# Sixteen tiles of an input projection by a form of Strassen's product, and two attention chains in lockstep

## The chip, the cores and the metric

One core of a Trainium2 chip runs the kernel. Five engines work from queues of their own: TensorE (PE) multiplies, VectorE (DVE), ScalarE (ACT) and GpSimd (POOL) work elementwise, SyncE (SP) issues the transfers. Semaphores order them. The metric is the time of one execution in device microseconds (us); lower is better. Before the change three runs gave 994.83 to 1002.69 us with a median of 996.45.

## The reference

One layer of a decoder trunk for 1024 tokens of width 1024: an input projection of the normed x, softmax attention on latents (MLA), gated linear attention (GLA) with 4 heads in chunks, a gated merge, an output product and gated embeddings.

```python
h = rmsnorm(x, norm_in_g[l])
proj = h @ w_in[l]
(cq, ckv, kr, gate_mla, gq, gk, gv, gk_low, gate_gla, merge_a, merge_b) = split_in(proj)
...
o_mla = mla_attention(q_nope, q_rope, k_nope, k_rope, v_mla).reshape(b, s, MLA_WIDTH)
y_a = (o_mla * jax.nn.silu(gate_mla)) @ w_mla_br[l]
...
o_gla = gla_chunked(qg, kg, vg, log_a).astype(x.dtype)
o_gla = rmsnorm(o_gla, gla_norm_g[l]).reshape(b, s, GLA_DV)
y_b = (o_gla * jax.nn.silu(gate_gla)) @ w_gla_br[l]
merged = jax.nn.sigmoid(merge_a) * y_a + jax.nn.sigmoid(merge_b) * y_b
x = x + merged @ w_out[l]
```

## The kernel before

Activations lie transposed, features on the 128 partitions and tokens along the row, in two halves of 512 tokens. Every float32 operand of a dense product is split into a high part that PE takes in one pass (fp32r) and the rest: `split` (L126) rounds the high part on ACT and subtracts on DVE. A product is then three matmuls, `mm3` (L144 to L147): high x high, and the two mixed ones; so all dense matmuls of the kernel stand in three lines.

The input projection has 33 tiles of 128 features. `stream` (L158) loads a tile's weights (`wr`, 512 KB, then `wh` and `wl`) one tile ahead; `bank` (L149) makes one PSUM bank of it: 8 k-tiles x 3 matmuls of 128x128 by 128x512, for one half of the tokens, so two banks of 24 a tile. An evict function takes the bank off PSUM times the tokens' rstd `rb` (L466): GG is GLA's gate (sg), GM the other gate, MA and MB the merge gates (stored to d_ta and d_tb in HBM), CKV and CQ the latents.

Linear attention, `gla(t, h)` (L531), works on head pair t and token half h in 11 steps: decayed keys and chunk states, then chunk scores transposed, level by level (exponents `level`, on DVE and ACT; `cross`, L559, 8 small matmuls into a two-bank tile L; `put`, L641, DVE's predicated copy into `at`), the outputs `o`, their norm, and the transposes `oT` back, multiplied into sg. The state runs from half 0 to half 1, so each head pair is a chain of two. `steps` (L733) runs the four one after the other, and after each of the 44 steps the loop asks `fill`, a stream of 29 of the tiles, for one bank. The rest of `fill` covers the splits of sg and the `finish_latent` (L757) of ckv and cq: broadcast of their norm's factor by PE (`dg`, `rb`) and 10 splits (`ch`, `cl`). Then come the softmax attention with `yb`, GLA's branch product, as filler, and the merge.

The written order gives priorities and data; a scheduler at build time fixes each engine's order, so the order of instructions is read from the built program. Work tiles come from 35 slots (`alloc`, `drop`, first in first out); a load waits on SP until its slot's last reader is done, and everything behind it on SP waits too.

```python
for _ in steps():
    next(fill)
    n_left -= 1
```

Of the kernel before, what the change touches and what calls it, by code (L numbers as in the profile page):

```python
# [8 lines left out]
F32 = mybir.dt.float32  # L9
# [42 lines left out]

def hybrid_kernel(tc, a, out):
# [3 lines left out]
    with ExitStack() as ctx:  # L57
# [7 lines left out]
        free = list(range(NSLOT))  # L65
        held = {}
        pools = [sp, None]
# [62 lines left out]
        def split_gain(dst_hi, dst_lo, src, g):  # L130
            """the two parts of src * g, g per partition"""
# [12 lines left out]
        def mm3(ps, lh, ll, rh, rl, first, last):  # L144
            nc.tensor.matmul(ps, lh, rh, start=first, stop=False)  # L145
            nc.tensor.matmul(ps, lh, rl, start=False, stop=False)  # L146
            nc.tensor.matmul(ps, ll, rh, start=False, stop=last)  # L147

        def bank(get, hi, lo, w, c0, kts, xh, xl, h, evict, tag="d"):  # L149
            """out[w features, half h of the tokens] with the weights' k-tiles at c0 + kt * w."""  # L150
            ps = get(tag, "d")
            n = len(kts)
            for i, kt in enumerate(kts):
                c = slice(c0 + kt * w, c0 + kt * w + w)
                mm3(ps[:w], hi[:, c], lo[:, c], xh[kt][:, hs(h)], xl[kt][:, hs(h)], i == 0, i == n - 1)
            evict(h, ps)

        def stream(get, jobs, xh, xl, primed=None, ahead=1, order=None):  # L158
# [17 lines left out]
            for n, h in order:  # L176
# [3 lines left out]
                bank(get, *ws[n], w, 0, range(nk), xh, xl, h, evict)  # L180
# [6 lines left out]
        def newton(dst, ss, n, w):  # L187
            """dst = rsqrt(ss / n + EPS), [128, w]"""
# [14 lines left out]
        def newton1(dst, s1, s2, n):  # L203
            """dst = rsqrt((s1 + s2) / n), [128, 1]; v is half the argument, the iterates change sign"""
# [13 lines left out]
        def rstd_rows(get, tag, acc, n, r):  # L218
            """From acc[128, tokens] (sums of squares by partition) the rstd of token block tb in r[128, 8]."""
# [5 lines left out]
        def rstd_parts(r):  # L225
            """both parts of r [128, 8]"""
# [5 lines left out]
        def rstd_bcast(get, tag, parts, h):  # L232
            """[128, 512] in PSUM: rstd of each token of half h along the free axis, on every partition."""
# [17 lines left out]
        d_rq = [[dr.tile([P, S], F32, name=f"d_rq{g}{y}") for y in range(2)] for g in range(2)]  # L251
        d_zb = [dr.tile([P, S], F32, name=f"d_zb{m}") for m in range(8)]
# [19 lines left out]
        with tc.tile_pool(name="ps0", bufs=1, space=PSUM) as ps0:  # L272
# [20 lines left out]
            # the array reaches its full clock only under load: it gets some while the first loads are on their way  # L293
# [4 lines left out]
            # x * g in two parts, and the sums of squares  # L298
            nc.sync.dma_start(wm0, a["w_misc"][:, 0 : NVEC + 128])
            xh, xl, xT = [], [], []  # L300
            acc = [alloc(F32, "xacc"), alloc(F32, "xacc")]
            first = stream(get, jobs, xh, xl)
            for k in range(8):
# [10 lines left out]
                xh.append(alloc(F32R, f"xh{k}"))  # L314
# [1000 lines left out]
```

## Time and profile before

| | |
|---|---|
| runs (3) | 994.83 to 1002.69 us, median 996.45 |
| profiled execution | span 995.6 us, 13955 instructions |
| PE busy | 968.8 us, 97% |
| DVE busy | 585.0 us, 59% |
| ACT, POOL busy | 413.4 us (42%), 127.8 us (13%) |
| longest wait of PE | 5.2 us, for kl in the softmax attention |

The span is the time from the first to the last instruction of the one profiled execution; the sum of the prediction is made against it. Busy times are unions over an engine's instructions. Matmuls run into one another, so a duration of one is longer than the time from its start to the next start. Idle time of PE in a stretch is the length less the busy time there.

### The profile page before, as it was taken

Reading aid. Unit: us, or ns where it says so; the run is one execution under the profiler, and the core shown is the slowest. Engines: PE = TensorE matmul, PEld = TensorE weight load, DVE = VectorE, ACT = ScalarE, POOL = GpSimd, SP = SyncE. Lnnn points to the kernel's source line nnn. Section 1 sums busy time; section 2 is a strip of 40 time slices with the busy share of each in tenths; the row PEclk is TensorE's granted clock in tenths of the full one; section 3 lists DMA queues with packets and bytes.
Section 4 is the critical chain, followed back from the end, with each engine's and each line's share of the span. In section 5 each row is a group of like instructions: output and inputs, shape, how many; then the busy total and the mean of one; then the engine's idle time right before and its main releaser. Section 6 shows DMA issues by size and latency. Waiting matters only on the chain. (4 is left out here: it accounts for less than half of the span.)

```text
span 995.6 us, 13955 instructions
## 1 busy us (share of the span) xinstructions
PE 968.8 (97%) x5152; PEld 801.1 (80%) x5152; DVE 585.0 (59%) x1219; ACT 413.4 (42%) x800; POOL 127.8 (13%) x103
## 2 busy tenths in 40 slices
PE   7999999999999999999999999997999999999996
PEld 5787778887887788788888788886888778889985
DVE  6727764375364355342567568885756862238766
ACT  7316721332331332221233246785886432237333
POOL 2100000000000000001111022234454000000322
PEclk9999999999999999999999999998999999999999
DMA  7300111122232122130162844537146762135212
GB/s 277 93 22 22 64 43 43 58 80 86 75 106 79 60 85 75 54 114 24 54 204 89 230 131 121 150 94 180 59 149 212 245 221 74 43 106 181 74 64 106
DMA packets 47827, 105.68 MB, mean 106 GB/s; under 512 B 6736, under 2 KB 9616, under 8 KB 47760
## 3 DMA queue, kind: packets, MB, share of 16 engines
q1 hardware_dynamic: 47760, 104.81, 32.9%
q8 instruction: 40, 0.66, 0.3%
q14 instruction: 27, 0.22, 0.1%
HBM read 72.18 MB, written 25.20 MB: 98 GB/s over the span
## 5 line engine op out<-in xcount | busy, mean ns | idle before, releaser
L145 PE MATMUL d<-xh,wh 128*128 128x512 f32 x544 | 215.4, 399 | 3.1 <-ACT xh L132 3.0
L146 PE MATMUL d<-xl,wh 128*128 128x512 f32 x544 | 214.1, 394 | 0.1
L147 PE MATMUL d<-xh,wl 128*128 128x512 f32 x544 | 213.8, 394 | 0.1
L145 PEld LDWEIGHTS d<-xh,wh 128*128 128x128 f32 x544 | 102.7, 189 | 28.2 <-ACT xh L132 4.9
L128 DVE TENSOR_TENSOR wl<-wr,wh 128x1024 fp32r<-128x1024 f32 (+2 forms) x59 | 73.6, 1249 | 86.9 <-ACT wh L127 66.7
L146 PEld LDWEIGHTS d<-xl,wh 128*128 128x128 f32 x544 | 102.9, 189 | 22.0 <-DVE xl L133 0.8
L147 PEld LDWEIGHTS d<-xh,wl 128*128 128x128 f32 x544 | 102.7, 189 | 22.2 <-DVE wl L128 0.5
L127 ACT ACTIVATE wh<-wr 128x1024 fp32r<-128x1024 f32 (+4 forms) x81 | 76.3, 943 | 105.5 <-DMA wr<-in_w_in 35.8
L145 PE MATMUL pg<-wh,gh 128*128 128x256 f32 (+1 forms) x200 | 62.7, 314 | 0.0
L146 PE MATMUL pg<-wl,gh 128*128 128x256 f32 (+1 forms) x200 | 62.5, 313 | 0.0
L147 PE MATMUL pg<-wh,gl 128*128 128x256 f32 (+1 forms) x200 | 62.5, 313 | 0.0
L128 DVE TENSOR_TENSOR pt<-pt,pt 128x512 fp32r<-128x512 f32 (+1 forms) x96 | 51.5, 551 | 16.1 <-ACT pt L127 15.7
L924 ACT ACTIVATE p<-p,nm 128x128 f32<-128x128 f32 (+3 forms) x64 | 49.3, 772 | 21.8 <-DVE nm L914 21.7
L494 ACT ACTIVATE z<-z 128x512 f32<-128x512 f32 x32 | 20.1, 629 | 91.1 <-DVE z L466 85.3
L466 DVE TENSOR_TENSOR z<-d,rb 128x512 f32<-128x512 f32 x32 | 22.0, 688 | 50.9 <-PE d L147 50.9
L145 PE MATMUL d<-mh,wh 128*128 128x512 f32 x128 | 50.9, 400 | 0.6 <-ACT mh L127 0.6
L127 ACT ACTIVATE pt<-pt 128x512 fp32r<-128x512 f32 (+1 forms) x96 | 44.6, 485 | 15.5 <-PE pt L963 14.0
L146 PE MATMUL d<-ol,wh 128*128 128x512 f32 x128 | 50.1, 393 | 0.4 <-DVE ol L128 0.4
L147 PE MATMUL d<-mh,wl 128*128 128x512 f32 x128 | 50.2, 392 | 0.0
L147 PE MATMUL d<-oh,wh 128*128 128x512 f32 x128 | 50.0, 392 | 0.0
L146 PE MATMUL d<-ml,wh 128*128 128x512 f32 x128 | 49.9, 390 | 0.0
L145 PE MATMUL d<-oh,wh 128*128 128x512 f32 x128 | 49.9, 395 | 0.0
(262 smaller groups left out, 1938.5 us busy)
## 6 DMA issues: line engine op xcount, KB each, us to landing
wr<-in_w_in SPq DMA_DIRECT2D x33, 512.0 KB
d_ta<-z SPq DMA_DIRECT2D x16, 256.0 KB
d_tb<-z SPq DMA_DIRECT2D x16, 256.0 KB
tb<-d_tb SPq DMA_DIRECT2D x16, 256.0 KB
d_zb<-tb SPq DMA_DIRECT2D x16, 256.0 KB
d_e<-er SPq DMA_DIRECT2D x16, 256.0 KB
ta<-d_ta SPq DMA_DIRECT2D x16, 256.0 KB
zb<-d_zb SPq DMA_DIRECT2D x16, 256.0 KB
```

The costliest lines, as they stand in the source:

```text
L127: nc.scalar.activation(dst_hi, src, AF.Copy)
L128: (eng or nc.vector).tensor_tensor(dst_lo, src, f(dst_hi), op=ALU.subtract)
L145: nc.tensor.matmul(ps, lh, rh, start=first, stop=False)
L146: nc.tensor.matmul(ps, lh, rl, start=False, stop=False)
L147: nc.tensor.matmul(ps, ll, rh, start=False, stop=last)
L466: nc.vector.tensor_tensor(z, ps, rb[:, hs(h)], op=ALU.mult)
L494: nc.scalar.activation(z, z, AF.Tanh, scale=0.5)
L924: nc.scalar.activation(pt[:, :w], pt[:, :w], AF.Exp, bias=nm, scale=-1.0, accum_out=den)
```

## The change

1. **Lockstep.** The chains of head pair 0 and head pair 1 run side by side, `zip(chain(0), chain(1))`: 22 double steps, with one fill bank after each but two. `fill` holds 13 tiles (GG 4, GM 4, MA 5).
2. **Strassen.** The other 16 tiles (MA 3, MB 8, CKV 2, CQ 3) go in 8 pairs through `strassen`. A pair is a 2x2 block product: tile 1 or 2 by first or second half of k (a11 to a22), times x by half of k and half of tokens (x11 to x22). Winograd's form makes 7 products instead of 8, each of 4 k-tiles x 3 matmuls, in four accumulators a to d in the order "abcbadc"; e is a copy of a after product 0. Weight sums (s1, s2, a11 - a21, a12 - s2) are made on POOL, x's sums once for all pairs by `operand_sums` (POOL and DVE) from a second load of x.
3. **sg by way of HBM.** sg is stored to d_sg as it becomes final (8 stores of 256 KB) and loaded again (4 of 512 KB) in the last pair, where its splits now stand.
4. **ckv and cq finish after Strassen**, without tiles of `fill` around them.
5. x's parts lie by half, high and low in one tile; their splits are 512 wide. Two more slots (6 for 4 of the second pool), 8 temporaries for 6, 9 of GLA's for 6. Comments are gone, so line numbers differ: dense matmuls stand in L146 to L148 afterwards, `cross` in L661.

```diff
-NMORE = 4
-NTMP = 6
-NG = 6
+NMORE = 6
+NTMP = 8
+NG = 9
...
+        def strassen(get, jobs, xs, ahead=4, done=None):
+            raws, sums, ws, st = {}, {}, {}, {}
+            W = HALF
+            def load(n):
+                if n < len(jobs):
+                    raws[n] = [alloc(F32, "wr") for _ in range(2)]
+                    for r, src in zip(raws[n], jobs[n][0]):
+                        nc.sync.dma_start(r, src)
+            def prep(n, j):
+                if n >= len(jobs):
+                    return
+                r1, r2 = raws[n]
+                a11, a12, a21, a22 = r1[:, :W], r1[:, W:], r2[:, :W], r2[:, W:]
+                if j == 0:
+                    sums[n] = alloc(F32, "ws")
+                s1, s2 = sums[n][:, :W], sums[n][:, W:]
+                ws[n, j] = alloc(F32R, "sw")
+                if j == 0:
+                    nc.gpsimd.tensor_tensor(s1, a21, a22, op=ALU.add)
+                    nc.gpsimd.tensor_tensor(s2, s1, a11, op=ALU.subtract)
+                    nc.gpsimd.tensor_tensor(a21, a11, a21, op=ALU.subtract)
+                if j == 6:
+                    nc.gpsimd.tensor_tensor(a12, a12, s2, op=ALU.subtract)
+                split(*pair(ws[n, j]), (a11, s2, s1, a21, a12, a22, a12)[j])
+                if j == 5:
+                    drop(r2)
+                    load(n + 1)
+                if j == 6:
+                    drop(raws.pop(n)[0], sums.pop(n))
+            def run(n, j):
+                b = "abcbadc"[j]
+                first = b not in st
+                if first:
+                    st[b] = get("w", "w" + b)
+                hi, lo = pair(ws[n, j])
+                for i in range(4):
+                    c = slice(i * P, (i + 1) * P)
+                    mm3(st[b], hi[:, c], lo[:, c], *pair(xs[j][i]), first and i == 0, i == 3, b != "d")
...
+                if j == 0:
+                    st["e"] = t2("e")
+                    nc.scalar.activation(st["e"], st["a"], AF.Copy)
+                elif j == 1:
+                    st["v"] = t2("v")
+                    nc.vector.tensor_tensor(st["v"], st["b"], st["e"], op=ALU.add)
+                elif j == 3:
+                    w_, z = t2("w"), t2("z22")
+                    st["u"] = w_
+                    nc.vector.tensor_tensor(w_, st["b"], st["e"], op=ALU.add)
+                    nc.vector.tensor_tensor(z, st["c"], w_, op=ALU.add)
+                    ev2(1, z)
...
-            jobs += [job(W_MA + m, ev_t(d_ta[m])) for m in range(8)]
-            jobs += [job(W_MB + m, ev_t(d_tb[m])) for m in range(8)]
-            jobs += [job(W_CKV + j, ev_ckv(j)) for j in range(2)]
-            jobs += [job(W_CQ + j, ev_cq(j)) for j in range(3)]
-            fill = stream(get, jobs, xh, xl)
+            jobs += [job(W_MA + m, ev_t(d_ta[m])) for m in range(5)]
+
+            order = [(n, h) for n in range(12) for h in range(2)] + [(12, 1), (12, 0)]
+            fill = stream(get_fill, jobs, xin, order=order)
...
-            for _ in steps():
-                next(fill)
-                n_left -= 1
-            drop(*bt, gci)
+            for n, _ in enumerate(zip(chain(0), chain(1))):
+                if n not in (5, 16):
+                    next(fill)
+            drop(*bt, gci, *sg)
...
+            def operand_sums(i):
+                r = raw.pop(i)
+                for n in range(2):
+                    nc.scalar.activation(r[n], r[n], AF.Copy, scale=col(V_IN + i + 4 * n))
+                x11, x12, x21, x22 = (r[n][:, hs(h)] for n in range(2) for h in range(2))
+                for q_ in tq:
+                    q_.append(alloc(F32R, "tq"))
+                nc.gpsimd.tensor_tensor(x11, x12, x11, op=ALU.subtract)
+                nc.vector.tensor_tensor(x12, x22, x12, op=ALU.subtract)
+                nc.gpsimd.tensor_tensor(x22, x22, x11, op=ALU.subtract)
+                nc.vector.tensor_tensor(x21, x21, x22, op=ALU.subtract)
+                for q_, x in zip(tq, (x11, x22, x12, x21)):
+                    split(*pair(q_[i]), x)
+                drop(*r)
...
+            xs = [xq[0][:4], tq[1], tq[0], tq[2], xq[0][4:], tq[3], xq[1][4:]]
+            pairs = strassen(get, jobs, xs)
+            for i in range(4):
                 next(fill)
+                operand_sums(i)
...
+                if j == 3:
+                    sg = [alloc(F32, f"sg{m}") for m in range(4)]
+                    oh, ol = [], []
+                    for m in range(4):
+                        nc.sync.dma_start(sg[m], d_sg[m])
+                        oh.append(alloc(F32R, "oh"))
+                        ol.append(alloc(F32R, "ol"))
+                        split(oh[m], ol[m], sg[m])
+                        drop(sg[m])
```

How the built program changes is shown at three places. A row is line, operation, output<-inputs and shape; the number at the end of a name tells one tile from the next; x_10_162 and the like are x's parts by half.

**The dense part of linear attention, PE, before:** d are banks of the fill, L the scores' tile of one chain.

```order
L145 MATMUL d_1158<-xh_34_211,wh_1005 128x512
L146 MATMUL d_1158<-xl_35_212,wh_1005 128x512
L147 MATMUL d_1158<-xh_34_211,wl_1006 128x512
L559 MATMUL L_163_1194<-r_162_1188 128x128 x8
L145 MATMUL d_1210<-xh_10_158,wh_1108 128x512
L146 MATMUL d_1210<-xl_11_159,wh_1108 128x512
L147 MATMUL d_1210<-xh_10_158,wl_1109 128x512
```

A cross of one chain stands between two banks, 24 matmuls from the next.

The same place after:

```order
L148 MATMUL d_1278<-x_35_230,wl_1073 128x512
L146 MATMUL d_1378<-x_10_162,wh_1212 128x512
L147 MATMUL d_1378<-x_10_162,wh_1212 128x512
L661 MATMUL L_180_1314<-r_179_1308 128x128 x8
L661 MATMUL L_182_1330<-r_181_1324 128x128 x8
L148 MATMUL d_1378<-x_10_162,wl_1213 128x512
L146 MATMUL d_1378<-x_13_172,wh_1212 128x512
L147 MATMUL d_1378<-x_13_172,wh_1212 128x512
```

Two crosses, one of each chain, stand together in a bank; the next two come 16 matmuls later.

**The end of linear attention, SP, before:** wr are weight loads, d_tb stores of the merge gate.

```order
L495 DMA d_tb_103<-z_3069 128x512
L495 DMA d_tb_104<-z_3137 128x512
L137 DMA wr_3352<-in_w_in 128x1024
L495 DMA d_tb_104<-z_3186 128x512
L137 DMA wr_3413<-in_w_in 128x1024
L495 DMA d_tb_105<-z_3235 128x512
```

The loads of the fill's next tiles stand between stores of its evicted banks.

After, at the entry into Strassen, wr_2716 and wr_2715 being tiles 2 and 1 of the first pair:

```order
L595 DMA d_ta_95<-z_2693 128x512
L207 DMA wr_2716<-in_w_in 128x1024
L824 DMA d_sg_130<-sg_114_899 128x512
L207 DMA wr_2715<-in_w_in 128x1024
L595 DMA d_ta_95<-z_2744 128x512
L207 DMA wr_2785<-in_w_in 128x1024
L207 DMA wr_2786<-in_w_in 128x1024
L207 DMA wr_2929<-in_w_in 128x1024
```

Stores of sg have come in between, and both loads stand behind stores; the first pair's tile 1 is behind the last store of sg.

DVE at the same place after (tq are the parts of x's sums, sw those of weights):

```order
L128 TENSOR_TENSOR tq_2553<-xr_2506,tq_2553 128x512
L823 SCALAR_TENSOR_TENSOR sg_114_899<-oT_2455,wm_71,sg_114_899 128x512
L128 TENSOR_TENSOR tq_2653<-xr_2514,tq_2653 128x512
L566 TENSOR_TENSOR z_2744<-d_2719,rb_139 128x512
L128 TENSOR_TENSOR sw_2782<-wr_2716,sw_2782 128x512
L128 TENSOR_TENSOR tq_2554<-xr_2505,tq_2554 128x512
L128 TENSOR_TENSOR sw_2749<-wr_2715,sw_2749 128x512
L128 TENSOR_TENSOR sw_2764<-wr_2715,sw_2764 128x512
```

The split of tq_2653, ahead of which sg_114 waits for oT_2455, frees the slot of wr_2715, whose split is sw_2749 four rows on.

**The finish of ckv, PE, before:** rb is the broadcast of the factors in dg.

```order
L145 MATMUL d_3606<-xh_25_193,wh_3479 128x512
L243 MATMUL rb_3547<-dg_3548,ones_r 128x512
L146 MATMUL d_3606<-xl_26_194,wh_3479 128x512
L147 MATMUL d_3606<-xh_25_193,wl_3480 128x512
L243 MATMUL rb_3547<-dg_3551,ones_r 128x512
L145 MATMUL d_3606<-xh_28_199,wh_3479 128x512
L146 MATMUL d_3606<-xl_29_200,wh_3479 128x512
L243 MATMUL rb_3560<-dg_3561,ones_r 128x512
```

The broadcasts stand singly among matmuls of the fill's last tiles. After (v are the attention's values, from ch and cl):

```order
L336 MATMUL rb_4071<-dg_4075,ones_r 128x512
L336 MATMUL rb_4087<-dg_4088,ones_r 128x512
L336 MATMUL rb_4087<-dg_4091,ones_r 128x512
L146 MATMUL v_4182<-wh_3989,ch_3913 128x512
L147 MATMUL v_4182<-wl_3990,ch_3913 128x512
L146 MATMUL v_4191<-wh_3989,ch_3913 128x512
L147 MATMUL v_4191<-wl_3990,ch_3913 128x512
L146 MATMUL v_4200<-wh_3989,ch_3913 128x512
L147 MATMUL v_4200<-wl_3990,ch_3913 128x512
L148 MATMUL v_4182<-wh_3989,cl_3915 128x512
```

The last three broadcasts follow one another, and the values' matmuls follow them directly; the tiles ahead are those of GLA's branch product.

## Rows read from the trace of the kernel before

**Rows 1.** Page: span, busy time of each engine, PE's busy tenths in 40 slices.
```profile
span 995.6 us, 13955 instructions
...
PE 968.8 (97%) x5152; PEld 801.1 (80%) x5152; DVE 585.0 (59%) x1219; ACT 413.4 (42%) x800; POOL 127.8 (13%) x103
...
PE   7999999999999999999999999997999999999996
```

**Rows 2.** Groups by line: count | busy us, mean ns of one | idle before.
```profile
L145 PE MATMUL d<-xh,wh 128*128 128x512 f32 x544 | 215.4, 399 | 3.1 <-ACT xh L132 3.0 <-ACT wh L127 0.2
```

**Rows 3.** Timeline of PE, 83.74 to 111.84 us: start, duration, instruction.
```profile
83.74 0.39 PE L147 MATMUL gv<-wh,xl 128*128 128x512 f32 x1
...
111.84 0.39 PE L145 MATMUL gv<-wh,xh 128*128 128x512 f32 x1
```

**Rows 4.** Stretches: length, busy time (count) by engine, PE's granted clock, DMA share, GB/s.
```profile
150.00:200.00 50.00, 50.00 (x256) 40.17 (x256) 22.14 (x37) 11.91 (x30) 2.41 (x3) 1.00 0.17 56
...
600.00:700.00 100.00, 92.21 (x529) 79.66 (x529) 76.85 (x221) 70.22 (x160) 35.77 (x24) 0.95 0.51 134
```

**Rows 5.** Waits of PE: what waited <- what for: total us, times, longest.
```profile
PE s L145 <- DMA kl<-kl: 5.2, 1, 5.2
PE d L145 <- ACT xh L132: 3.0, 3, 2.5
```

**Rows 6.** Timeline of PE around one cross.
```profile
148.67 1.16 PE L559 MATMUL L<-r 64*128 64x128 f32 x16
149.76 0.50 PE L145 MATMUL d<-xh,wh 128*128 128x512 f32 x1
```

**Rows 7.** Timeline of DVE: a put and its successor.
```profile
150.84 1.34 DVE L641 COPY_PREDICATED at<-gci,L 128x1024 f32<-128x1024 int32 x1
152.07 0.41 DVE L667 TENSOR_TENSOR rk<-gqkv,dd 128x256 f32<-128x256 f32 x1
```

**Rows 8.** Groups by line: 512-wide operations of POOL, DVE and ACT.
```profile
L521 POOL TENSOR_TENSOR latents<-latents,csq 128x512 f32<-128x512 f32 x6 | 8.0, 1334 | 76.2 <-ACT csq L520 76.2
...
L128 DVE TENSOR_TENSOR cl<-latents,ch 128x512 fp32r<-128x512 f32 x10 | 6.3, 683 | 0.0
L127 ACT ACTIVATE ch<-latents 128x512 fp32r<-128x512 f32 x10 | 6.3, 632 | 9.1 <-DVE latents L769 8.9
```

**Rows 9.** Timeline of all engines: a weight load's issue and its first reader.
```profile
390.76 0.33 SPq L137 DMA_DIRECT2D wr<-in_w_in  x1
...
394.69 1.06 ACT L127 ACTIVATE wh<-wr 128x1024 fp32r<-128x1024 f32 x1 [2.34 <-DMA wr<-in_w_in]
```

**Rows 10.** Timeline of all engines: a DVE split alone, and beside a POOL sum.
```profile
10.73 1.28 DVE L133 SCALAR_TENSOR_TENSOR xl<-xT,wm,xh 128x1024 fp32r<-128x1024 f32 x1 [0.36 <-ACT xh L132]
...
16.21 2.41 POOL L334 TENSOR_TENSOR xacc<-xacc,xT 128x1024 f32<-128x1024 f32 x1 [15.24 <-ACT xT L332]
...
17.21 2.50 DVE L133 SCALAR_TENSOR_TENSOR xl<-xT,wm,xh 128x1024 fp32r<-128x1024 f32 x1 [0.97 <-ACT xh L132]
```

**Rows 11.** Stretches of PE around its longest gap: length, busy time, granted clock.
```profile
686.00:690.00 4.00, 0.00 (x0) 1.00 1.02 241
690.00:691.00 1.00, 0.42 (x1) 0.68 0.97 250
691.00:700.00 9.00, 8.63 (x33) 0.50 0.56 173
700.00:702.00 2.00, 2.00 (x14) 0.85 0.20 71
```

**Rows 12.** Timeline of PE: the two longest gaps behind the first 25 us.
```profile
562.14 0.64 PE L145 MATMUL s<-kh,qh 96*128 96x128 f32 x3 [1.47 <-issue]
...
690.33 0.42 PE L145 MATMUL s<-kh,qh 96*128 96x128 f32 x1 [5.17 <-DMA kl<-kl]
```

**Rows 13.** Timeline of SP: issues ahead of that gap.
```profile
683.79 0.42 SPq L137 DMA_DIRECT2D wr<-in_pT  x1
...
685.87 0.65 SPq L864 DMA_DIRECT2D kl<-kl  x1
```

More of the change, by code (lines that the diff above doesn't have):

```diff
@@ L65, in hybrid_kernel @@
         free = list(range(NSLOT))
+        pools = [sp, None]
         held = {}
-        pools = [sp, None]
         count = [0]
@@ L142, in load_w, with mm3, halves, pair @@
             return hi, lo
[L144 to L149, printed above, removed]
+        def mm3(ps, lh, ll, rh, rl, first, last, more=False):
+            nc.tensor.matmul(ps, lh, rh, start=first, stop=False, skip_group_check=more)
+            nc.tensor.matmul(ps, lh, rl, start=False, stop=False, skip_group_check=more)
+            nc.tensor.matmul(ps, ll, rh, start=False, stop=last, skip_group_check=more)
+        def halves(xh, xl):
+            return lambda kt, h: (xh[kt][:, hs(h)], xl[kt][:, hs(h)])
+        def pair(t):
+            return t[:, 0:HALF], t[:, HALF:S]
+        def bank(get, hi, lo, w, c0, kts, x, h, evict, tag="d"):
             ps = get(tag, "d")
@@ L179, in stream @@
                     fetch()
-                bank(get, *ws[n], w, 0, range(nk), xh, xl, h, evict)
+                bank(get, *ws[n], w, 0, range(nk), x, h, evict)
                 left[n] -= 1
@@ L183, in stream @@
                     drop(*ws.pop(n))
+                yield
+        def strassen(get, jobs, xs, ahead=4, done=None):
[36 more added lines that the diff above has]
+                    mm3(st[b], hi[:, c], lo[:, c], *pair(xs[j][i]), first and i == 0, i == 3, b != "d")
+                drop(ws.pop((n, j)))
+                _, ev1, ev2 = jobs[n]
+                if j == 0:
[10 more added lines that the diff above has]
+                    ev2(1, z)
+                elif j == 4:
+                    ev1(0, st["a"])
+                elif j == 5:
+                    z = st["u"]
+                    nc.vector.tensor_tensor(z, st["d"], z, op=ALU.add)
+                    ev2(0, z)
+                elif j == 6:
+                    z = st["v"]
+                    nc.vector.tensor_tensor(z, st["c"], z, op=ALU.add)
+                    ev1(1, z)
+                    st.clear()
+            load(0)
+            yield
+            for q in range(ahead):
+                prep(*divmod(q, 7))
+            yield
+            for q in range(7 * len(jobs)):
+                prep(*divmod(q + ahead, 7))
+                run(*divmod(q, 7))
+                if done:
+                    done(*divmod(q, 7))
@@ L251, in hybrid_kernel @@
         d_rq = [[dr.tile([P, S], F32, name=f"d_rq{g}{y}") for y in range(2)] for g in range(2)]
+        d_sg = [dr.tile([P, S], F32, name=f"d_sg{m}") for m in range(4)]
         d_zb = [dr.tile([P, S], F32, name=f"d_zb{m}") for m in range(8)]
@@ L344, in hybrid_kernel @@
             for h in range(2):
-                bank(get, *w0, P, 0, range(8), xh, xl, h, ev_misc)
+                bank(get, *w0, P, 0, range(8), xin, h, ev_misc)
             drop(*w0)
@@ L782, in ev_yb @@
                 return ev
-            yb = stream(lambda *x: getB[0](*x), [(a["w_gla_br"][m * P : (m + 1) * P, :], P, 4, ev_yb(m)) for m in range(8)], oh, ol)
-            for n in range(n_left - 5):
-                next(fill)
-            kvh, kvl = finish_latent(get, "o", "L", "ckv", 256, V_KV)
-            next(fill)
-            next(fill)
-            next(fill)
+            yb = stream(lambda *x: getB[0](*x), [(a["w_gla_br"][m * P : (m + 1) * P, :], P, 4, ev_yb(m)) for m in range(8)], halves(oh, ol))
+            kvh, kvl = finish_latent(get, "d", "d", "ckv", 256, V_KV)
             next(yb)
-            for _ in fill:
-                pass
-            drop(*xh, *xl, rb)
         with tc.tile_pool(name="psB", bufs=1, space=PSUM) as psB:
@@ L831, in rope_queries @@
                 for h in range(2):
-                    bank(get, hi, lo, P, 0, range(3), qh, ql, h, ev)
+                    bank(get, hi, lo, P, 0, range(3), halves(qh, ql), h, ev)
                     yield
@@ L858, in make_pair @@
                     for h in range(2):
-                        bank(get, hi, lo, P, c0, range(n), xh_, xl_, h, ev(x))
+                        bank(get, hi, lo, P, c0, range(n), halves(xh_, xl_), h, ev(x))
                         yield
```

87 lines of the change are left out of this document (58 added, 29 removed).

## The prediction

> **What bounds the kernel now.** I read the shares of the span first: TensorE (PE) is busy 97% of 995.6 us, VectorE (DVE) 59%, and of the forty slices only the first, one in the attention and the last fall below 9 for PE [rows 1]. The mean of a 128x512 matmul, 399 ns [rows 2], is no price, since neighbours overlap. Two starts give one: from 83.74 to 111.84 us PE issued 124 such matmuls without a gap, so one takes (111.84 - 83.74) / 124 = 0.2266 us and a bank of 24 takes 5.44 [rows 3]. Then the busy time by stretch: in 150 to 200 us, the linear attention with its fill, PE is busy all 50 us; 600 to 700 lacks 7.8 [rows 4]. Last PE's waits: the two longest are 5.2 us for kl in the softmax attention and 3.0 for xh at the start [rows 5]. So where the change is made, 110 to 550 us, PE hardly waits: a matmul that goes away there is worth its issue time, and a wait that comes in is paid in full.
>
> **What it removes.** A pair of two w_in tiles took 2 x 2 x 24 = 96 matmuls and takes 7 x 12 = 84; 8 pairs save 96 matmuls of 128x512, all else on PE keeping its count. At 0.2266 us: -21.8 us. By the mean duration it would be 38; I reject that for the overlap.
>
> **Lockstep and 26 fill banks.** Before, the chains' 44 steps took one bank each; now 22 double steps take 20. In the dense part the order shows two crosses, 16 matmuls, two crosses. A cross moves the next matmul from 148.67 to 149.76 us, 1.09 [rows 6], so a double level comes every 16 x 0.2266 + 2 x 1.09 = 5.8 us. DVE has two puts in it, 152.07 - 150.84 = 1.23 us each [rows 7]; an eviction and an sg product, 0.68 long [rows 8] and about 0.6 from start to start (the put is 1.34 long and its successor starts after 1.23); and up to three of 256 columns, 0.41 long [rows 7], at 0.33: 4.7 us, in one gap of three 1.2 more for a weight split. Most exponents of levels 8, 4 and 2 stand ahead of the puts, so walked by these prices each put ends 1.3 us or more before the cross that needs it. I take 0. The upper end is one put late at each of the 2 x 4 double levels, 8 x 1.23 = 10 us.
>
> **The entry into Strassen.** The last fill bank ends 12 matmuls (2.7 us) after the last oT. The first product needs a11 in wr_2715. Its load stands on SP behind the store of the last sg and waits for a slot that one of DVE's splits frees right behind that sg: 0.4 us until the transposes are done [rows 2], sg and split at 0.6, so the issue is 1.6 us after oT. Such a load reached ScalarE 394.69 - 390.76 = 3.93 us after its issue [rows 9]; a high and a low part at about 0.6 each (0.63 and 0.68 long [rows 8]) make 6.8 us after oT, against 2.7: 4.1 us of idle PE. Product 1 + 4 then accumulates on the same bank, which ScalarE must first have copied to e: 0.4 until the matmuls are done and 0.6, so 1.1 us with the semaphore. Third, GpSimd (POOL) starts s2 = s1 - a11 when DVE wants a11's low part. The trace has such a meeting: the split xl took 1.28 us alone and 2.50 when it began 1.00 us into a 2.41 us sum on POOL; it ended 1.09 after that sum [rows 10]. A sum of 512 columns takes 1.33 [rows 8]; I add a quarter, 0.3. Together 5.5 us. Bounds: 0 (the slot comes free earlier), and 4.1 + 1.1 + 2 x 1.33 = 7.9.
>
> [...]
>
> **Pairs 2 to 8.** A pair is 84 x 0.2266 = 19.0 us on PE. DVE has 7 low parts, 4 evictions and 4 combinations, 15 x 0.6 = 9.0; ScalarE 7 high parts, e and evictions, some 12 x 0.6 = 7; POOL 4 x 1.33 = 5.3. DVE and POOL one after the other are 14.3 of 19.0. Later weights are loaded when an earlier pair's first product ends and are used 72 matmuls (16 us) on; less 3.9 of landing and 1.2 of splitting, 11 remain. What can wait is a bank that is evicted and taken again (b after v, c after z22), covered where another product stands between. Bounds 0 and 7 x (0.4 + 0.6) = 7; I take 1, nearer to nothing, as the order has other products between in most pairs.
>
> **Operand sums, d_sg, splits.** 8 loads of x (512 KB), 8 sums each on POOL and DVE and 16 splits fall into the last four fill banks, 21.8 us of PE. DVE's 24 x 0.6 = 14 us and POOL's 10.7 fit beside it; what is late of them is the slot above. The 8 stores and 4 reloads of sg queue on SP only. The split of x by halves at the start: 0, half a us either way.
>
> **The tail.** Before, the broadcast of ckv's factor and its splits had fill between them (rb among d banks in the order); now only yb's first tiles and the last product stand there. DVE has then the low parts of the gated outputs, weight splits, 8 dg, 10 latents and 10 cl; by the prices above cl is some 1.2 us late for the first v and 0.8 for the first d behind it. I take 2. Bounds: 0, and 8 x 0.6 = 5 if the gated outputs' low parts all stand in front uncovered.
>
> **The sum.** 995.6 - 21.8 + 0 + 5.5 + 1 + 0 + 2 = 982.3 for the span. The median of the runs, 996.45, is 0.85 above the profiled span, so 983.
>
> **The rivals.**
> (a) *All hidden*: wr_2715's slot is free early and the tail is covered: 996.45 - 21.8 + 1 = 976. For it: two more slots. Against: the load waits for that very split.
> [...]
> [...]
> (c) *The attention's gap moves.* kl's issue stands on SP behind other loads (in_pT at 683.79, kl at 685.87 [rows 13]), and the new order puts in_ple_g ahead of it too. Gone with its half clock: 983 - 10 = 973. Twice: 993.
> (d) *The lockstep starves PE*: 993 with all eight double levels, 988 with four.
> (e) *Weights just in time: slower.* If slots came free only with a pair's last products, each of 8 pairs would wait 3.9 + 1.2 us less a product's cover of 1; past 21.8 / 8 = 2.7 us a pair it eats the gain, and at 4.1 us it gives 983 - 5 + 8 x 4.1 = 1011. Against: the release 16 us ahead.
> (f) *Whole sums hold the entry's splits*: 983 + 2 x 1.33 - 0.3 = 985.
> [...]
>
> **Chances.** Forecast (978 to 987) 0.44, (a) 0.12, (b) 0.12, (c) 0.06 down and 0.04 up, (d) 0.05, (e) 0.05, (f) 0.08, (g) 0.04. The range takes in (a), (c) down, (b), (f) and (d): 971 to 993, and leaves out (e), (g) and part of (c) and (d). One per cent, about what a measurement of this kernel can tell from no change, is 986.5 and 1006.4: faster is the forecast but for its top, (a), (c) down and (f), 0.42 + 0.12 + 0.06 + 0.08 = 0.68; same 0.27 from the top, (b), (c) up, (d) and (g); slower (e), 0.05.
>
> **What would show it.** Right: 96 fewer 128x512 matmuls; pairs 19 us apart; one PE wait of 3 to 6 us at the first wa, one of about 1 for e, 1 to 2 on cl; DVE's busy time up by 112 x 0.68 less 16 weight splits of two times 0.6, 585 to about 640 us. Wrong: PE waits on sw in each pair (e), on DVE's at ahead of crosses (d), a clock under 1.00 behind the first wa (b), no wait on sw (a), kl's wait gone or doubled (c).

## The result, and the profile after

The changed kernel takes 1004.8 us (median of 14 runs) against 997.5 for the kernel before beside it: a ratio of 1.0066, 95% interval 1.0046 to 1.0087. The forecast was 983 with a range of 971 to 993; the kernel became 0.7% slower, and the forecast was wrong by about 22 us.

The page after: span, busy time, PE's busy tenths and its granted clock.

```profile
span 1003.2 us, 14056 instructions
...
PE 954.2 (95%) x5056; PEld 790.0 (79%) x5056; DVE 654.1 (65%) x1330; ACT 453.0 (45%) x879; POOL 191.4 (19%) x143
...
PE   8899999999989799999999999898999999999996
PEclk9989999999989999999999999988999999999998
```

PE has 96 matmuls fewer and is busy 14.6 us less, yet the span is 7.6 us longer: it now idles 49.0 us where it idled 26.8 [rows 1]. DVE's 654 us are 14 above the forecast of 640. PE's waits after (what waited <- what for: total us, times, longest):

```profile
PE s L146 <- DMA kh<-kh: 5.3, 3, 2.2
PE rb L336 <- DVE dg L330: 4.7, 1, 4.7
PE wa L146 <- ACT sw L127: 4.2, 1, 4.2
...
PE s L147 <- DMA kl<-kl: 2.7, 3, 1.4
...
PE d L146 <- DVE vp L128: 1.6, 1, 1.6
...
PE v L148 <- DVE cl L128: 0.8, 1, 0.8
```

Of these the sum had wa's wait for sw and, in the tail, one for cl and one of the first d behind it. The one wait of before on kl [rows 5] has become many small ones on kh and kl and, further down, on nm and pt. The clock fell with them; stretches of PE after (length, busy time, granted clock, DMA share, GB/s):

```profile
292.00:298.00 6.00, 5.59 (x14) 0.54 0.00 0
...
334.00:340.00 6.00, 4.33 (x12) 0.72 0.14 51
558.00:566.00 8.00, 6.24 (x26) 0.79 1.00 216
606.00:612.00 6.00, 5.44 (x23) 0.72 0.48 131
650.00:660.00 10.00, 7.53 (x34) 0.66 0.45 116
694.00:704.00 10.00, 6.72 (x24) 0.66 0.71 181
```

In the kernel before one such stretch stood behind one gap [rows 11]; now there are six and one more at 48 to 56 us. To see where the time went, both programs are cut at the same four tiles of PE's timeline: the first gv (the start is over), the first kdT (linear attention begins), the first v (the projection is done) and the last s (the last scores); the last pg ends the table. The stretch from gv to kdT is 45.0 us in both and is left out. Us of the profiled execution:

| | to first gv | kdT to first v | first v to last s | last s to last pg |
|---|---|---|---|---|
| before | 70.9 | 405.1 | 204.7 | 259.8 |
| after | 76.4 | 393.4 | 218.7 | 259.9 |
| difference | +5.5 | -11.8 | +14.0 | +0.1 |

The stretch that the change rewrites gained 11.8 us. The gain was lost in two others: the start, for which the sum had 0, and first v to last s, for which it had only the tail's 2 (the tail's waits for cl and vp come behind the first v).

### The profile page after: what moved, and what is told of

Its sections match the earlier page's. It is cut to its first block, busy times and chain, and to the rows that moved or that the text cites. A ratio compares the mean times of both kernels' runs of the same rounds, so it can differ in the third digit from the quotient of the medians.

```text
span 1003.2 us, 14056 instructions
## 1 busy us (share of the span) xinstructions
PE 954.2 (95%) x5056; PEld 790.0 (79%) x5056; DVE 654.1 (65%) x1330; ACT 453.0 (45%) x879; POOL 191.4 (19%) x143
## 4 chain that ended last, share of the span: by engine, by line
PE 74%; DVE 8%; DMA 7%; ACT 5%; issue 2%; POOL 2%; SPq 1%; POOLq 0%; DVEq 0%; ACTq 0%
PE d L146 11%; PE d L147 11%; PE d L148 11%; PE pg L148 3%; PE pg L146 3%; PE pg L147 3%; PE pt L1118 2%; PE L L661 2%; PE s L147 2%; PE s L148 2%; PE s L146 2%; PE wc L146 1%; PE o L1110 1%; PE wc L148 1%; PE wb L148 1%
## 5 line engine op out<-in xcount | busy, mean ns | idle before, releaser
L146 PE MATMUL d<-x,wh 128*128 128x512 f32 x288 | 115.6, 408 | 5.9 <-ACT wh L127 3.3
L147 PE MATMUL d<-x,wh 128*128 128x512 f32 x288 | 115.9, 403 | 0.0
L148 PE MATMUL d<-x,wl 128*128 128x512 f32 x288 | 114.6, 399 | 0.4 <-DVE wl L128 0.3
L127 ACT ACTIVATE wh<-wr 128x1024 fp32r<-128x1024 f32 (+4 forms) x65 | 59.1, 913 | 81.4 <-DMA wr<-in_w_gv 11.3
L128 DVE TENSOR_TENSOR wl<-wr,wh 128x1024 fp32r<-128x1024 f32 (+2 forms) x43 | 50.7, 1181 | 40.9 <-ACT wh L127 21.8
L146 PEld LDWEIGHTS d<-x,wh 128*128 128x128 f32 x288 | 55.8, 194 | 20.6 <-ACT x L132 4.9
L148 PEld LDWEIGHTS d<-x,wl 128*128 128x128 f32 x288 | 55.3, 192 | 13.0 <-DVE wl L128 1.0
L147 PEld LDWEIGHTS d<-x,wh 128*128 128x128 f32 x288 | 55.9, 194 | 12.0 <-issue 0.2
L146 PE MATMUL pg<-wh,gh 128*128 128x256 f32 (+1 forms) x200 | 62.6, 313 | 0.0
L148 PE MATMUL pg<-wh,gl 128*128 128x256 f32 (+1 forms) x200 | 62.6, 313 | 0.0
L1371 POOL TENSOR_TENSOR x<-x,fg 128x512 f32<-128x512 f32 x16 | 20.7, 1298 | 191.1 <-ACT g L1343 191.1
L146 PE MATMUL d<-oh,wh 128*128 128x512 f32 x128 | 50.3, 397 | 2.5 <-ACT oh L127 2.5
L148 PE MATMUL d<-oh,wh 128*128 128x512 f32 x128 | 50.6, 397 | 0.0
L146 PE MATMUL d<-mh,wh 128*128 128x512 f32 x128 | 50.5, 398 | 0.0
L148 PE MATMUL d<-mh,wl 128*128 128x512 f32 x128 | 49.8, 391 | 0.0
L1069 DVE CUSTOM_DVE_ANT_0 p<-s,cm 128x512 f32<-128x512 f32 (+2 forms) x64 | 37.0, 586 | 17.7 <-PE s L148 15.9
```

The lines of the kernel that those rows point to most:

```text
L127: nc.scalar.activation(dst_hi, src, AF.Copy)
L128: (eng or nc.vector).tensor_tensor(dst_lo, src, f(dst_hi), op=ALU.subtract)
L146: nc.tensor.matmul(ps, lh, rh, start=first, stop=False, skip_group_check=more)
L147: nc.tensor.matmul(ps, lh, rl, start=False, stop=False, skip_group_check=more)
L148: nc.tensor.matmul(ps, ll, rh, start=False, stop=last, skip_group_check=more)
L1069: nc.vector.tensor_tensor_reduce(out=pt[:, c], in0=st, in1=cmask[:, S - cw : S] if c.stop == w else cmask[:, 0:cw], scale=-SCALE, scalar=l ...
```

## The experiments

Two theories: A, lockstep and Strassen pay about what was forecast, and the time is lost outside, at the start and in the softmax attention; B, the attention and the rest suffer from what Strassen leaves behind or Strassen gains nothing. Twelve kernels ran. Ratios are to the kernel before run beside them; the columns are those of the table above.

| run | median us | ratio (95%) | to gv | kdT to v | v to last s |
|---|---|---|---|---|---|
| e1_sum_on_dve | 1002.8 | 1.005 (1.003 to 1.008) | 71.8 | 393.7 | 220.8 |
| e2_halves_only | 999.8 | 1.001 (0.999 to 1.003) | 75.2 | 405.1 | 206.2 |
| e3_lockstep_only | 994.9 | 0.997 (0.994 to 1.000) | 70.9 | 408.8 | 204.1 |
| e4_no_strassen | 1012.7 | 1.014 (1.010 to 1.018) | 74.2 | 400.8 | 218.5 |
| e6_before_two_more_slots | 1004.1 | 1.007 (1.004 to 1.010) | 70.9 | 405.1 | 211.4 |
| e7_after_four_slots | 993.5 | 0.997 (0.995 to 0.999) | 76.4 | 394.3 | 207.4 |
| e8_four_slots_and_sum | 991.8 | 0.995 (0.993 to 0.997) | 73.3 | 394.4 | 212.3 |
| e9_and_early_weights | 990.9 | 0.994 (0.992 to 0.996) | 73.8 | 390.1 | 214.2 |
| e10_filler_in_gap | 1002.3 | 1.005 (1.003 to 1.007) | 70.6 | 405.2 | 213.0 |
| e11_best_with_filler | 995.1 | 0.999 (0.996 to 1.001) | 72.4 | 390.9 | 212.7 |
| e12_lag_two_steps | 996.9 | 1.000 (0.999 to 1.002) | 71.2 | 404.8 | 205.2 |
| e13_best_with_lag | 995.9 | 1.000 (0.997 to 1.002) | 72.8 | 396.8 | 209.7 |

### The start: the sum on GpSimd

```diff
-                    eng = nc.gpsimd if k % 2 == 0 else nc.vector
+                    eng = nc.gpsimd if k in (2, 4) else nc.vector
```

> The changed kernel with one edit: the last of GpSimd's three sums of squares at the start (1024 columns) is done by VectorE. Theory A (that sum, which took 8.58 us in the changed kernel against 3.36 before, is held off by VectorE's unbroken row of splits, and weights, factor and broadcast wait behind it): the first gv matmul comes at about 72 us instead of 76.45, the 4.67 us wait of PE on dg goes below 1 us, and the time falls by 4 to 5 us unless the attention is reordered. Theory B (the broadcast is late because of weight loads from HBM): first gv stays at 76 us, time unchanged.

And the reverse, the kernel before with nothing but the half-wide splits:

```diff
-                if k == 0:
-                    for h in range(2):
-                        split_gain(xh[k][:, hs(h)], xl[k][:, hs(h)], t[:, hs(h)], col(V_IN + k))
+                for h in range(2):
+                    split_gain(xh[k][:, hs(h)], xl[k][:, hs(h)], t[:, hs(h)], col(V_IN + k))
...
-                else:
-                    split_gain(xh[k], xl[k], t, col(V_IN + k))
```

> The kernel before with one edit: all splits of x at the start are made by halves of 512 columns, as in the changed kernel. Theory A (the half-wide splits let VectorE hold off GpSimd's sum): GpSimd's third sum takes 6 to 9 us instead of 3.36 and the first gv moves from 70.93 to 75 or 76 us; time 4 to 5 us longer. Theory B (the start is late for another reason than the splits): first gv stays near 71 us and the time is that of before.

The second and the third sum on POOL in the changed kernel, DVE beside them, and PE's wait (timelines: start, duration):

```profile
20.69 2.96 POOL L429 TENSOR_TENSOR xacc<-xacc,xT 128x1024 f32<-128x1024 f32 x1 [0.39 <-ACT xT L427]
...
21.31 6.20 DVE L133 SCALAR_TENSOR_TENSOR x<-xT,wm,x 128x512 fp32r<-128x512 f32 x6
27.43 1.21 DVE L128 TENSOR_TENSOR wl<-wr,wh 128x1024 fp32r<-128x1024 f32 x1
...
28.00 8.58 POOL L429 TENSOR_TENSOR xacc<-xacc,xT 128x1024 f32<-128x1024 f32 x1 [4.34 <-ACT xT L427]
...
28.57 1.21 DVE L429 TENSOR_TENSOR xacc<-xacc,xT 128x1024 f32<-128x1024 f32 x1
29.71 2.35 DVE L128 TENSOR_TENSOR wl<-wr,wh 128x1024 fp32r<-128x1024 f32 x2
31.98 1.21 DVE L429 TENSOR_TENSOR xacc<-xacc,xT 128x1024 f32<-128x1024 f32 x1
33.11 1.21 DVE L128 TENSOR_TENSOR wl<-wr,wh 128x1024 fp32r<-128x1024 f32 x1
...
50.36 2.60 PE L336 MATMUL rb<-dg,ones_r 128*128 128x512 f32 x4 [4.67 <-DVE dg L330]
```

POOL's third sum is issued at 28.00, when DVE has a row of operations in hand, and ends at 36.58, 2.26 us after DVE's row does at 34.32. That is nearly the 2.41 us that such a sum took before [rows 10], so it seems to have done its work after DVE's last operation. Before, DVE was the one held up: 2.50 us instead of 1.28 for a split, and two weight splits in 4.56 us beside POOL's third and slowest sum:

```profile
26.63 3.36 POOL L334 TENSOR_TENSOR xacc<-xacc,xT 128x1024 f32<-128x1024 f32 x1 [2.32 <-ACT xT L332]
...
27.65 4.56 DVE L128 TENSOR_TENSOR wl<-wr,wh 128x1024 fp32r<-128x1024 f32 x2
```

In e2:

```profile
27.90 7.45 POOL L332 TENSOR_TENSOR xacc<-xacc,xT 128x1024 f32<-128x1024 f32 x1 [4.35 <-ACT xT L330]
```

In e1 PE's wait on dg is 0.7 us and the first gv comes 4.7 us earlier. At the start both experiments came out as Theory A has it, from both sides: half-wide splits alone cost 4.2 us, and taking the sum away gives 4.7 back. The times show less of it: e2's median is 2.0 us longer (1.001, no change that can be told, and its profile is the longest of its ten runs), and e1's is 2.0 shorter, not 4 to 5, its profile being 2.1 longer in the attention.

That the half-wide splits cost this is shown; why POOL loses is not. It is not that DVE's operations beside the sum are shorter: those are sums and weight splits 1024 wide, of 1.21 us, as before. Beside half-wide splits POOL did not lose: its second sum took 2.96 us, and DVE's six splits 6.20, where six in the same program took 4.06 ahead of it. What the edit changes is the time at which the third sum meets DVE's row: 28.00 (27.90 in e2) instead of 26.63.

### Lockstep alone, and the change without Strassen

```diff
-            for _ in steps():
+            for _ in zip(chain(0), chain(1)):
                 next(fill)
                 n_left -= 1
```

> The kernel before with the two chains of linear attention in lockstep (one bank of fill per double step, 9 temporaries of its own instead of 6); all tiles by the plain product. Theory A (lockstep costs PE nothing, and its doubled blocks of small matmuls save some changes of shape): the stretch from the first kdT to the first v, 405.1 us before, becomes 399 to 405. Theory B (lockstep starves PE at the levels): 410 or more. The softmax attention may come out in another order; its stretch is read by itself.

```diff
-            jobs = [((p_[0], q_[0]), p_[1], q_[1]) for p_, q_ in zip(ts[::2], ts[1::2])]
...
-            pairs = strassen(get, jobs, xs)
+            plain = stream(get, ts, xin)
```

> The changed kernel with its 16 Strassen tiles by the plain product (96 more matmuls, no sums of x, no sums of weights, sg still by way of HBM, latents still finished after the tiles). Theory A (Strassen saves 21.8 us and loses some 9 to its entry, 4.4 + 1.7 + 1.3 of waits and 1.6 of half clock): the stretch from the first kdT to the first v, 393.4 us in the changed kernel, becomes 404 to 408. Theory B (what Strassen saves it loses on its other engines): 393 to 398.

e4's 400.8 lies between the theories. Against the changed kernel's 393.4, Strassen nets 7.5 of its 21.8 us. The other 14.3 are in rows of the changed kernel: PE's waits for sw, e, z and one weight split,

```profile
292.41 0.80 PE L146 MATMUL d<-x,wh 128*128 128x512 f32 x1 [3.15 <-ACT wh L127]
...
335.67 0.80 PE L146 MATMUL wa<-x,sw 128*128 128x512 f32 x1 [4.19 <-ACT sw L127]
341.55 0.50 PE L146 MATMUL wa<-x,sw 128*128 128x512 f32 x1 [1.54 <-ACT e L245]
359.38 0.47 PE L146 MATMUL wc<-x,sw 128*128 128x512 f32 x1 [1.17 <-DVE z L253]
```

10.1 us in all, of which e4 keeps 0.7 (its wait on wh), and up to 2.8 and 1.7 of slow clock behind the first two (0.54 and 0.72 over 6 us): together up to 13.9. The 3.15 us are the sums of x at work: the weights had been on their way since 257.92, but ScalarE stood at the scaling of x, whose load was late, with the weights' split behind it.

```profile
288.47 1.15 ACT L879 ACTIVATE xr<-xr,wm 128x1024 f32<-128x1024 f32 x1 [3.44 <-DMA xr<-in_xT]
...
291.32 1.04 ACT L127 ACTIVATE wh<-wr 128x1024 fp32r<-128x1024 f32 x1
```

Lockstep with everything else but Strassen (e4) has 400.8 against 405.1 before, 4.3 shorter. PE changes between dense and small matmuls 113 times in that stretch before and 75 times in the changed kernel. By the starts before, where dense matmuls follow at 0.2266 us, the step into a row of small ones takes 0.05 us more on the mean (the cross at 148.67 starts 0.32 behind the dense one ahead) and the step behind the first dense one afterwards 0.09 more (149.76 to 150.10), so 38 changes fewer, if e4 has no more than the changed kernel, are some 2.6 us, an estimate. e3 has 408.8, in a profile in which the clock fell while PE was busy, some 3 us behind a wait of 0.55 us:

```profile
270.00:284.00 14.00, 13.45 (x129) 1.00 0.01 1
284.00:286.00 2.00, 2.00 (x10) 0.87 0.00 0
286.00:304.00 18.00, 18.00 (x52) 0.50 0.00 0
```

PE was then in one row of 32 o pairs, 128 columns each; rows of it, with the clock at full and at half:

```profile
284.75 0.48 PE L700 MATMUL o<-st,qe 64*128 64x128 f32 x2
285.17 0.52 PE L684 MATMUL o<-gqkv,at 128*128 128x128 f32 x2
...
290.68 0.79 PE L684 MATMUL o<-gqkv,at 128*128 128x128 f32 x2
291.41 0.79 PE L700 MATMUL o<-st,qe 64*128 64x128 f32 x2
```

18 us at half and 2 at 0.87 are at most 9.3 us lost. By the starts of the pairs, 0.42 us apart before the fall and 0.72 behind it, 25 pairs lost about 7.5 (an estimate from these starts). Without the loss the stretch has 399.5 to 401.3, the lower end of Theory A's range. The clock does not fall so far in each execution: of e3's ten runs six have a mean granted clock of 0.989 or more and take 989.4 to 995.5 us, the other four have 0.982 or less and take 998.9 or more.

### The attention: two more slots

The attention's code is untouched, but its order is not: of PE's and DVE's rows from the first to the last s little more than half stand in the sequence of before. The order came out in one of two forms in all builds but those with filler matmuls (and, by a few rows, e13), and what goes with the one or the other is the number of work slots, 4 or 6 in the second pool.

```diff
-NMORE = 4
+NMORE = 6
...
-    nc = bacc.Bacc("TRN2", target_bir_lowering=False, num_devices=1)
+    nc = bacc.Bacc("TRN2", target_bir_lowering=False, num_devices=1, dynamic_dma_scratch_size=1024)
```

> The kernel before with two more work slots in its second pool (6 instead of 4, and the smaller descriptor space that makes room for them); nothing else. Its softmax attention then has PE and DVE orders that are row for row those of the changed kernel. Theory A (the attention's loss comes from the order that two more slots give): first v to last s, 204.7 us before and 218.7 in the changed kernel, becomes 214 to 220, and the time 1006 to 1012. Theory B (the attention suffers from what the Strassen stage leaves behind, its transfers or later loads): 204 to 206, time 996 to 999.

And in the changed kernel:

```diff
             drop(rb)
+            del free[:2]
```

> The changed kernel with two slots taken out of the list of free ones when the Strassen pairs are done, so that the attention has as many as before; its attention's PE and DVE orders are then row for row those of the kernel before. Theory A: first v to last s falls from 218.7 to 204 to 207, time 990 to 993 instead of 1004.8. Theory B (the Strassen stage itself hurts the attention): it stays at 216 to 219, time 1002 to 1005.

e6, which has no lockstep and no Strassen, is as slow as the changed kernel (1.0071 against 1.0066), and e7, which has both, loses its slowdown: 993.5 us, a ratio of 0.997 instead of 1.007, by one line. The smaller descriptor space in e6 is not the cause: e3 and e12 have it too, with 204.1 and 205.2 us and the order of before. Theory B falls as the main cause, and e4 speaks against it as well, which has the long order, no Strassen and 218.5 us (5.6 of them a wait for vp). But e6's 211.4 and 1004.1 us lie below what Theory A gave (214 to 220, 1006 to 1012), so the order alone is not the whole 14.0. PE's gaps at the changes of head pair, in the changed kernel,

```profile
605.37 0.47 PE L146 MATMUL s<-kh,qh 96*128 96x128 f32 x2 [1.76 <-DVE pt L128]
...
628.20 0.51 PE L146 MATMUL s<-kh,qh 128*128 128x512 f32 x1 [0.99 <-DVE nm L1069]
...
651.05 0.64 PE L146 MATMUL s<-kh,qh 96*128 96x128 f32 x3 [1.36 <-DMA kh<-kh]
653.74 0.47 PE L147 MATMUL s<-kl,qh 96*128 96x128 f32 x1 [1.42 <-DMA kl<-kl]
...
697.22 0.77 PE L146 MATMUL s<-kh,qh 96*128 96x128 f32 x2 [2.21 <-DMA kh<-kh]
```

in e6, which has the same order (the first three again),

```profile
610.29 0.47 PE L145 MATMUL s<-kh,qh 96*128 96x128 f32 x2 [1.31 <-DVE pt L128]
...
631.37 0.51 PE L145 MATMUL s<-kh,qh 128*128 128x512 f32 x1 [0.93 <-DVE nm L914]
...
654.23 0.67 PE L145 MATMUL s<-kh,qh 96*128 96x128 f32 x3 [1.38 <-DMA kh<-kh]
```

and in e7 (all above 0.6 us behind 600 us):

```profile
645.51 0.33 PE L147 MATMUL s<-kl,qh 96*128 96x128 f32 x1 [0.71 <-DMA kl<-kl]
687.77 0.44 PE L146 MATMUL s<-kh,qh 96*128 96x128 f32 x1 [3.47 <-DMA kl<-kl]
688.93 0.44 PE L147 MATMUL s<-kl,qh 96*128 96x128 f32 x1 [0.71 <-DMA kl<-kl]
```

The waits of the long order come with the order. From first v to last s PE is idle 16.2 us in the changed kernel and 10.9 in e7, 13.8 in e6 and 9.6 before. In the changed kernel the rest is mostly clock. The last four stretches shown in the first section lose at most 8 x 0.21 + 6 x 0.28 + 10 x 0.34 + 10 x 0.34 = 10.2 us to it (at most, since PE is idle in part of them). The kernel before loses 1 x 0.32 + 9 x 0.50 + 2 x 0.15 = 5.1 behind its last gap alone [rows 11], and e7 some 5 as well: its mean granted clock, 0.983 over 991.2 us for 0.978 over 1003.2 in the changed kernel, makes 5.2 us less lost in all. e6 loses no more than that, 1.7 behind a wait for vp, none at the third pair and 3.4 at the last:

```profile
690.00:710.00 20.00, 16.43 (x89) 0.83 0.62 172
```

So the order costs 6.7 us in e6 and 11.3 in the changed kernel against e7, whose 2.7 over before are nearly the tail's two waits (0.85 for cl and 1.63 for vp there). Why the clock falls more often with that order in the changed kernel than in e6, and why two slots more make the scheduler choose it, was not pursued.

### Put together

e8 is e7 with e1's edit.

> The run before (two slots taken out for the attention) and the third sum of squares on VectorE. Theory A (both losses add up): first gv at 72, first v to last s 204 to 207, time 985 to 988. If the losses only move: 990 or more.

e9 loads the first pair's weights ahead of x's sums:

```diff
+            next(pairs)
             for i in range(4):
                 next(fill)
+                if i == 3:
+                    drop(*xq[1][:4])
                 operand_sums(i)
-            next(pairs)
             next(fill)
-            drop(*xq[1][:4])
...
-NG = 9
+NG = 7
```

> The run before and the first pair's weights loaded ahead of the sums of x (the first half of the other token half's parts given back one bank earlier, 7 temporaries of the linear attention instead of 9, else it does not fit). Theory A (the entry's waits, 4.2 for sw and 1.5 for e with 1.6 of half clock, come from the late load): PE's wait on the first wa goes below 1 us and the stretch from last oT to last w shortens by 4 to 7 us; time 979 to 983. Theory B (the parts of x's sums are late too): the wait moves to wb on tq, shorter by less than 3 us; time 983 to 987.

e9 is the fastest, 990.9 us and 0.6% under the kernel before, but both miss what Theory A gives, by 4 and by 8 us. e8 gets only 3.1 of the 4.7 us at the start (dg's wait is 1.66 us). In e9 the stretch from the last oT to the last w is 3.3 us shorter than in e8 and not 4 to 7, since part of the entry's wait moved to the second product, nearly as Theory B has it (its time, 990.9, lies above both theories'):

```profile
332.54 0.50 PE L146 MATMUL wb<-tq,sw 128*128 128x512 f32 x1 [2.15 <-ACT sw L127]
334.11 0.79 PE L148 MATMUL wb<-tq,sw 128*128 128x512 f32 x1 [0.79 <-DVE sw L128]
```

And the attention takes 212 and 214 us in the order that takes 204.7 before and 207.4 in e7; e9's profile has a wait of 2.4 us for kh at the first scores and of 5.6 for kl at the last pair's. The two profiles are among the longest of their runs (995.1 us where the median is 991.8, 993.5 where it is 990.9), which may be part of it. So part of the loss in the attention does not hang on the order and stays open.

### The clock in the gap, and the lag

```diff
+                n_fill = {3: 18}.get(pr, 0)
+                if n_fill:
+                    pw = get("d", "warm")
+                    kk_ = qk["kh", 2 * pr + 1]
+                    for _ in range(n_fill):
+                        nc.tensor.matmul(pw, kk_[64:128, 512:640], kk_[64:128, 0:HALF], start=True, stop=True)
                 drop(hi, lo)
```

> The kernel before with 18 matmuls of 64x128 by 128x512 more (4.1 us of PE), whose result nothing reads, placed ahead of the last head pair's first scores, where PE stands idle for 5.2 us and the granted clock is 0.50 for some 9 us behind it. Theory A (the clock falls because of the idle stretch, and its fall costs 5 us besides): kl's wait shrinks to about 1 us, the clock stays 1.00 behind it, and the stretch from first to last s, 163.6 us, becomes 158 to 160; time 3 to 5 us shorter, although PE does more. Theory B (the clock falls there for another reason, or the work behind the filler is late instead): the stretch is 163 to 168 and the time the same or up to 4 us longer.

> The last run of the series (four slots in the attention, third sum on VectorE, first pair's weights early) with such matmuls ahead of the first (8) and the last head pair's scores (18). Theory A: first to last s, 169.8 us there, becomes 162 to 165 and the stretch ahead of it, with a slow clock from 554 to 565, 1 to 3 us shorter; time 983 to 987. Theory B: 990 or more.

Both are some 4 us slower than without the filler, e10 by slightly more than Theory B gave, with 170.4 us from first to last s. e10's gap at the last pair is gone, and the clock fell all the same, with a wait of DVE's rc behind it. Gaps of e10, and its clock:

```profile
693.90 0.44 PE L960 MATMUL o<-pt,vp 128*128 128x384 f32 x1 [0.89 <-ACT pt L127]
695.34 0.41 PE L146 MATMUL s<-kl,qh 96*128 96x128 f32 x1 [0.93 <-DMA kl<-kl]
704.69 0.37 PE L945 MATMUL rcT<-ident,rc 128*4 128x128 f32 x1 [2.75 <-DVE rc L933]
```

```profile
686.00:694.00 8.00, 7.11 (x35) 1.00 0.78 188
...
696.00:702.00 6.00, 5.94 (x20) 0.50 0.72 194
```

Filling PE there buys nothing. The likely reason, not shown by itself, is that the filler's 4.1 us stand ahead of work that DVE and ScalarE wait for. It is not the only difference: at the first pair, where no filler stands, the wait grew from 1.47 us to 2.94 and the clock fell behind it as well (562 to 570 us), which stays open. So the 5.1 us of half clock behind the gap of 5.17 before [rows 11, 12], which rival (c) took off together with it, do not go away with the gap.

```diff
-            for _ in zip(chain(0), chain(1)):
+            c0, c1 = chain(0), chain(1)
+            for n in range(22 + 2):
+                next(c0, None)
+                if n >= 2:
+                    next(c1, None)
```

> The kernel with lockstep alone, but the second chain two steps behind the first, so that the four groups of o matmuls of a half stand apart in PE's order instead of in one row. In the run without the lag PE's granted clock was 0.50 from 286 to 304 us although PE was busy all that time, from the moment when that row of 32 pairs of small matmuls had begun. Theory A (a long row of small matmuls alone lets the clock fall): no clock under 0.9 between 270 and 320 us, first kdT to first v 398 to 402 us instead of 408.8, time 5 to 9 us shorter than there. Theory B (the short wait of 0.55 us ahead of them did it, or chance): 405 to 410, the clock still falls.

> The best version so far (two slots taken out for the attention, third sum on VectorE, first pair's weights early: 990.9 us) with the same lag of two steps, still 20 fill banks beside the chains. Its clock did not fall in the linear attention, so Theory A expects no gain but what VectorE's freer row gives at the levels: 988 to 991. If lag costs (PE waits for the second chain at its end, 2 banks fewer): 992 to 996.

In e12 the clock stays up where it had fallen (270 to 296 us: busy 26.00 of 26.00 at 1.00), so it is the run of o groups in one piece that went with the fall; with one profile of each, chance is not excluded. But the stretch is 404.8, not 398 to 402, and the median, 996.9, is not shorter than e3's. What lockstep had saved is gone, in part because PE waits 2.5 us there (0.8 in e3) and in part, it seems, because fewer blocks of the two chains stand together: PE changes between dense and small matmuls 89 times in that stretch and 75 times in e3, 1.0 us at the mean prices above. e13 is 5 us slower than e9, at the upper end of what was expected if lag costs: PE waits for z and for at at the levels (2.5 and 2.0 us) and for the first pair's sw (3.4).

## Why the prediction was wrong

**What it removes** was right: 96 matmuls fewer, and no long wait in the pairs behind the first.

**Lockstep**, taken at 0 with an upper end of 10: no put was late in the changed kernel. Lockstep with all else but Strassen made the stretch 4.3 us shorter (e4), of which the fewer changes between dense and small matmuls are some 2.6 by estimate; and in e3's profile a half clock took 7.5 to 9.3 that the sum had no term for. Rival (d), starving at the levels, did not happen.

**The entry**, 5.5 us with 4.1 for sw and 1.1 for e, measured 4.19 and 1.54, besides up to 1.7 of slow clock (0.72 over 334 to 340 us), the sign of rival (b): the step that held best, in part by luck. The load was issued later than summed (0.7 us after the store of the last sg, and 2.3 after the transposes' issue where the sum had 1.6), and the first product needed only the high part, 0.7 us after ScalarE began it where the sum had 1.2 for both parts. Whole sums holding splits, rival (f), cost PE nothing there: two low parts of sw took 2.90 us beside POOL's sums where two took 1.29 just before, but they came behind PE's wait for sw, which was 4.19 against the 4.1 summed without any hold. **Pairs 2 to 8** took their 1: 1.17 for z, once. **The tail**, 2 us, measured 0.84 for cl and 1.62 for vp.

**Operand sums** were called hidden because DVE's 14 and POOL's 10.7 us fit beside four banks. The capacity was right, the queue was not looked at: ScalarE's scaling of x waited for a late load and held the fill's weight split behind it, 3.15 us and up to 2.8 of clock. The prediction followed the queues of SP and DVE behind a wait and not ScalarE's.

The whole stretch came out at -11.8 against -21.8 + 5.5 + 1 = -15.3, since this 5.9 and the entry's 1.7 of clock stand against the 4.3 that e4 shows for the rest of the change.

**The split of x by halves at the start**, "0, half a us either way", is the first step that failed: +5.5 us at the first gv, 4.2 of it shown by that edit alone (e2). The trace of before had such a meeting of DVE and POOL in [rows 10], and I used it at the entry for 0.3 us; I did not ask which of the two is held when the sum meets DVE's row at another moment.

**The attention** was not a term at all, only rival (c) for one gap. This is the step that decided the sign: +14.0 us with the tail's 2.5, and 11.3 of them go when the two slots are taken out again (e7). The change to it is the constant NMORE, which rival (a) counted as a help ("two more slots"). The order of the changed program shows it over the whole attention; the prediction read there only SP's rows ahead of one gap.

All in all: -11.8 + 5.5 + 14.0 = +7.7, which is the 7.6 of the spans. The sum had -15.3, 0 and 2 for the three, so it missed by 3.5, 5.5 and 12.0 us. Slower had a chance of 0.05, all of it for rival (e), and that rival's waits for sw in each pair did not come: no rival had the two stretches that made it slower.

## What to carry to other kernels

When a scheduler builds the order, compare the order of every long stage, also of those whose code is untouched: a pool's size is an edit to all of them, and here it cost about what the rewritten stretch gained (11.3 and 11.8 us). Where two engines hold each other up (a split of DVE took 2.50 us for 1.28 before [rows 10], a sum of POOL 8.58 after), ask which of them wins at the new times, do not take it from one old meeting, and follow the loser's result to the chain that waits for it. A saving in instructions on the bound engine is paid out only as far as the other engines' queues stay clear of waits at the entry (here 7.5 of 21.8 us); each wait there is priced with what stands behind it in the queue.

## What the runs showed of the hardware

- GpSimd was held off by VectorE for a whole row of operations: a sum of 128x1024 that took 2.41 us before [rows 10] took 8.58 us beside six back-to-back operations of DVE, and 7.45 in e2. In the kernel before, beside such a sum, a split of the same width on DVE was the one held, 2.50 us where it took 1.28 alone [rows 10]; what decides between them is not shown.
- The granted clock was 0.50 for 18 us (286 to 304 us) in which PE was busy throughout, in a row of 128-column matmuls (e3); with the row cut into pieces of eight pairs (e12) it stayed at 1.00 from 270 to 296 us. It fell in e10 behind gaps of 0.89 and 0.93 us (0.50 from 696 to 702) although the long gap ahead had been filled.
- Gaps of 1.36 to 1.76 us (ending at 559.95, 605.37 and 651.05 us after) were followed by stretches at a mean granted clock of 0.79, 0.72 and 0.66 (the stretches from 558, 606 and 650 us of the first section), where one of 1.47 before [rows 12], one of 1.72 in e12 (ending at 562.37) and one of 2.98 in e13 (at 560.76) were followed by 1.00: the length of the gap alone does not tell.
